# W_o and x kept in halves; attention results of two tiles loaded and combined before the projections end

## Chip, cores and metric

The kernel runs on one core of one Trainium2 chip. The metric is the device time of one execution in microseconds (us), the median of several runs.

## The reference

One inference step of a decoder layer: 2048 prompt rows (x_prompt) and 32 sample rows (8 requests of 4), width 1024. What matters here is the path from x to the mixer's output:

```python
qa, ka, va, qb, kb, vb, ga, gb = jnp.split(x @ w_in, SPLIT_POINTS, axis=-1)
# A: window 128, 8 query heads; B: (window, dilation) (128,1), (512,4), (2048,16)
oa = _band_values(p, va).reshape(n, t, A_Q)          # softmax with sinks
ob = _combine_groups(outs, lses)                     # three dilations, weighted by denominators
m = jax.nn.sigmoid(ga) * (oa @ w_br_a) + jax.nn.sigmoid(gb) * (ob @ w_br_b)
mix = m @ w_o
h = _layernorm(ALPHA * x + mix, ln1_g, ln1_b)
...
a = sum((conv_w[j] * ext[:, j:j + t] for j in range(CONV_W)), conv_b)
f = (jax.nn.gelu(a, approximate=False) * v) @ w_down
```

The sample rows attend to caches that are read from HBM. All is float32; outputs are the two y, the new cache rows and the convolution states.

## The kernel before

Every float32 operand of a product is split into a high part (ACT copies it, rounded) and a low part (DVE or GpSimd, called POOL, subtracts): `split`, lines 41 and 42. A product is then three matmuls, high by high, low by high and high by low.

**Phase 1** projects x. x is loaded, transposed on TensorE (PE) and kept whole in SBUF as one tile R, 128 partitions x 8 blocks of the width x 2048 rows. The work is a list of slots, `seq` in `phase1`, one slot per tile of 128 rows and per kind: B0, B1 and B2 (the three dilations of B), A, and G (the gates' last columns). The rows of a tile are a slice of R's columns: contiguous for B0, A and G, with stride 4 for B1 and stride 16 for B2. Each kind has 16 slots and one slot for the sample rows (number 16, which in G stands after slot 2). A slot runs four weight units of 256 columns (tile w), 96 matmuls into two banks psd (line 383); `make_xs` splits the x of the next slot (tile xs) at the slot's start. The banks are evicted by ACT (line 454, into a buffer b) in G and stored to d_gate by POOL's queue.

Everything else is threaded between the matmuls, eight points a slot: attention of the slot before, in G the sample attention (`sample_attn`, tiles V), and `wsteps`, a list of splits of the weights that come next. `pace` says how many splits run at each point (2 in G). Raw weights pass through the ten buffers b (`bufp`): `prefetch` issues their loads on SP up to `rawlim` pieces ahead, each of 256 KB, in a fixed order: w_in, then W_o in 16 pieces, the branch weights br in 12 (w_br_a's left half, w_br_b, w_br_a's right half, four each), then w_up. `loadcap` bounds how far. A split releases its buffer, and its step issues the next load.

**The passage to phase 2.** After G slot 13 `phase2_begin` opens the pool p2a and loads the attention results of tile 0: `load(0)` is nine DMAs on SP (oa; rb, the reciprocal denominators, into a buffer b; the weights wb; ob of the three dilations, strided) and `loadg` two (the gates ga). In slot 14, after the first unit, R is released and its place taken by WO (`phase2_weights`), 16 pieces to be split; after the third unit tile 0 is combined (`combine`: DVE weights and adds the dilations) and split into oT. In slot 15 the branch weights are split into the w tiles that the slot's units release; after its third unit come `load(1)` and the first sigmoids.

**Phase 2** goes over 16 prompt tiles and the sample tile: `mT(i-1)` transposes the gated sum m, `branches(i)` multiplies oT by the branch weights (four groups, 36 matmuls into psb, line 1089), DVE multiplies by the gates (line 1234) and POOL adds (line 1240, m), `oT(i+1)` is split, `outproj(i-1)` multiplies by WO (48 matmuls into psw, line 1089), and the layer norm follows. `combine(i+1)` stands in `branches(i)` between the gate products of its first and its second half. `load(i+1)` is issued at the start of iteration i. The tiles oa, wb, ob and oT have one buffer each, so load(i+1) waits until oT(i) has been made, and oT(i+1) until branches(i) has been read. **Phase 3** is the ConvFFN (psu, psdn) in four groups of rows.

Engines run in the order in which the program issues; SP's queue too.

Of the kernel before, what the change touches and what calls it, by code (L numbers as in the profile page):

```python
# [7 lines left out]
F32 = mybir.dt.float32  # L8
F32R = mybir.dt.float32r
# [7 lines left out]
SEQ = 2048  # L17
# [17 lines left out]
class Net:  # L35
# [142 lines left out]
    def phase1(self):  # L178
        nc, tc, a = self.nc, self.tc, self.a
        with ExitStack() as st:  # L180
            rp = ExitStack()
# [5 lines left out]
            self.R = self.pool(rp, "rp").tile([128, 8, SEQ], F32, name="R")  # L187
# [35 lines left out]
            for n, (kind, i, t) in enumerate(seq):  # L223
# [4 lines left out]
                self.pool_gate = kind == "G"  # L228
                nxt = seq[n + 1] if n + 1 < len(seq) else None
# [32 lines left out]
                if kind == "G" and i == 13:  # L262
                    assert not self.jobs, "sample attention is late"
                    sa.close()
                    self.phase2_begin()
                if kind == "G" and i in (12, 13):
                    if i == 12:
                        cc = self.conv_consts()
                    next(cc, 0)
# [61 lines left out]
    def trans_x(self, i):  # L331
        nc = self.nc
        xr = self.xr.pop(i)
        for h in range(2):
            ps = self.psT.tile([128, 512], F32, tag="t", name="pst")
            for k in range(4):
                nc.tensor.transpose(ps[:, k * 128:(k + 1) * 128], xr[h][:, k * 128:(k + 1) * 128], self.idn)
            nc.scalar.activation(self.R[:, 4 * h:4 * h + 4, i * 128:(i + 1) * 128],
                                 ps.rearrange("p (k t) -> p k t", k=4), AF.Copy)
# [9 lines left out]
    def make_xs(self, t, pool=False):  # L349
        xs = self.xsp.tile([128, 2, 8, 128], F32R, tag="xs", name="xs")  # L350
        self.split(xs[:, 0], xs[:, 1], self.R[:, :, t[1]], self.nc.gpsimd if pool else None)
        return xs

    def slot(self, kind, i, t, xs, units, prep, after_unit, rp):
        nc = self.nc
# [10 lines left out]
        if kind == "A" and i == 16:  # L366
            pace = (0, 0, 1, 1, 1, 1, 2, 2)
        if kind != "B0" or i > 0:
            out = prep()
        for half in range(2):  # L370
            ps = self.pd.tile([128, 512], F32, tag="d", name="psd")
            for uu in range(2):
# [23 lines left out]
                if u == 0 and kind == "G" and i == 14:  # L396
                    rp.close()
                    self.phase2_weights()
                after_unit(u)
                if kind == "G" and i == 14 and u == 2:  # L400
                    self.combine(0)
                    self.oT(0)
                if kind == "G" and i == 15 and u == 2:
                    self.load(1)
                if kind == "G" and i == 15 and u == 2:
                    self.sigmoid(0)
# [692 lines left out]
    def phase2_begin(self):  # L1099
        self.sta = ExitStack()  # L1100
        self.p2a = self.pool(self.sta, "p2a", side="right")
        self.S = {}
        self.load(0)
        self.loadg(0, 0)
        self.loadg(0, 1)

    def phase2_weights(self):

        self.wost = ExitStack()
        self.WO = self.pool(self.wost, "wop").tile([128, 2, 8, 1024], F32R, name="WO")  # L1110
        for c in range(4):
            cs = slice(c * 256, c * 256 + 256)
            self.wsteps += self.unit_steps((self.WO[:, 0, :, cs], self.WO[:, 1, :, cs]), True)[1]
# [7 lines left out]
    def load(self, i):  # L1121
# [3 lines left out]
        if M == 128:  # L1125
            d["oa"] = self.p2a.tile([128, 4, 128], F32, tag="oa", name="oa")
            nc.sync.dma_start(d["oa"], self.d_oa[:, r0:r0 + M].rearrange("(k p) t -> p k t", p=128))
            rb = self.buf()
            d["rb"] = rb.rearrange("p (c t) -> p c t", c=4)
# [65 lines left out]
    def phase2(self):  # L1195
# [17 lines left out]
        def branches(i):  # L1213
# [4 lines left out]
            for n in range(2):  # L1218
# [24 lines left out]
                if n == 0 and i < N - 1:  # L1243
                    self.combine(i + 1)
# [13 lines left out]
        def outproj(i):  # L1258
# [4 lines left out]
            for n in range(2):  # L1263
                cs = slice(n * 512, (n + 1) * 512)
                ps = psW.tile([128, 512], F32, tag="w", name="psw")
                for k in range(8):
                    self.split_mm(ps, M, t[:, 0, k], t[:, 1, k], WO[:, 0, k, cs], WO[:, 1, k, cs], k == 0, k == 7)
# [384 lines left out]
```

## Time and profile before

| | us |
|---|---|
| median of 3 runs | 3225.4 (3224.82 to 3226.73) |
| the profiled execution | 3227.46 |
| its span, first to last instruction | 3225.7 |
| PE busy with matmuls | 3157.8 (98%) |
| DVE busy | 1813.1 (56%) |
| ACT busy | 1419.3 (44%) |
| POOL busy | 747.1 (23%) |

PE's busy time is modelled to a matmul's end, so it doesn't tell full speed from a lower clock; the granted clock does, 0.994 in the mean of the span. Phase 1 ends at about 1297 us, phase 2 lies from 1299 to 1673, phase 3 behind. A row of a timeline gives start, duration, engine, line, operation, output and inputs; in brackets the idle time before it and what ended that. SPq is SP's queue of DMA issues.

### The profile page before, as it was taken

To read this page: it belongs to the slowest core of one execution; us is meant where nothing else is said; L and a number is where in the kernel's file an instruction comes from. 1 tells how busy PE (TensorE), PEld (TensorE's weight loads), DVE (VectorE), ACT (ScalarE), POOL (GpSimd) and SP (SyncE) were. 2 spreads that over 40 slices of the span, in tenths; PEclk is the share of its full clock that TensorE was granted. 3 is DMA by queue.
4 is the path that set the end of the run, shared out by engine and by line. 5 is a ranking of instruction groups with operands and counts; after the bars stand their busy time and mean duration, and the time that the engine had idled before them with its cause. 6 is when DMAs were issued, how large, how long until landed. Compare 5 with 4: busy or idle time off the path is not lost.

```text
span 3225.7 us, 56679 instructions
## 1 busy us (share of the span) xinstructions
PE 3157.8 (98%) x21839; PEld 2909.1 (90%) x21839; DVE 1813.1 (56%) x3694; ACT 1419.3 (44%) x3257; POOL 747.1 (23%) x783
## 2 busy tenths in 40 slices
PE   8999999999999999899999999999999999999998
PEld 8999998998999899688877988888888988999998
DVE  5656656656676532677765444564446444474446
ACT  6666666666666442322224233342343242342332
POOL 2114544654332201355540000020003000030001
PEclk9999999999999999899999999999999999999999
DMA  3113313413221344877735323443334333442231
GB/s 117 55 49 96 85 33 103 122 52 101 70 62 49 89 153 124 211 184 181 189 120 151 98 88 95 132 141 91 100 107 116 125 98 92 127 142 83 71 98 54
DMA packets 480548, 343.03 MB, mean 106 GB/s; under 512 B 114450, under 2 KB 436076, under 8 KB 480278
## 3 DMA queue, kind: packets, MB, share of 16 engines
q1 hardware_dynamic: 462390, 290.78, 31.7%
q0 software_dynamic: 17744, 48.56, 5.1%
q8 instruction: 172, 2.82, 0.4%
q14 instruction: 98, 0.80, 0.1%
q10 hardware_dynamic: 144, 0.07, 0.0%
HBM read 279.71 MB, written 59.59 MB: 105 GB/s over the span
## 4 chain that ended last, share of the span: by engine, by line
PE 67%; issue 6%; DVE 4%; ACT 3%; DMA 2%; POOL 1%; SPq 0%; DVEq 0%; POOLq 0%; ACTq 0%
PE psu L1411 31%; PE psdn L1089 14%; PE psd L383 8%; PE psw L1089 5%; PE psb L1089 4%; PE psdf L1089 1%; ACT P L721 1%; DVE w L42 1%; PE pst L566 1%; DMA oa<-d_oa 1%; PE pso L736 1%; DVE P L716 0%; PE pst L1253 0%; DVE b L575 0%; PE pss L636 0%
## 5 line engine op out<-in xcount | busy, mean ns | idle before, releaser
L1411 PE MATMUL psu<-h,w 128*128 128x512 f32 (+1 forms) x5280 | 1012.4, 353 | 2.8 <-ACT h L41 2.8
L383 PE MATMUL psd<-w,xs 128*128 128x256 f32 x7680 | 978.1, 284 | 21.1 <-DVE w L42 7.1
L1411 PEld LDWEIGHTS psu<-h,w 128*128 128x128 f32 x5280 | 860.3, 188 | 149.3 <-ACT h L41 3.8
L383 PEld LDWEIGHTS psd<-w,xs 128*128 128x128 f32 x7680 | 935.9, 190 | 28.2 <-ACT w L41 10.2
L1089 PE MATMUL psdn<-w,gt 128*128 128x256 f32 (+1 forms) x4008 | 474.9, 279 | 1.9 <-DVE y L1462 1.9
L1089 PEld LDWEIGHTS psdn<-w,gt 128*128 128x128 f32 (+1 forms) x4008 | 472.2, 186 | 4.9 <-DVE y L1462 4.1
L42 DVE TENSOR_TENSOR w<-b,w 128x512 fp32r<-128x512 f32 (+1 forms) x613 | 406.8, 722 | 19.2 <-ACT w L41 18.1
L41 ACT ACTIVATE w<-b 128x512 fp32r<-128x512 f32 x636 | 346.0, 607 | 126.5 <-PE psdn L1089 61.1
L1422 ACT ACTIVATE ext<-psu 128x512 f32<-128x512 f32 (+1 forms) x110 | 56.3, 512 | 452.1 <-PE psu L1411 452.0
L1435 DVE SCALAR_TENSOR_TENSOR ac<-ext,cw,ac 128x512 f32<-128x512 f32 (+1 forms) x88 | 71.2, 809 | 286.9 <-ACT ac L1434 286.9
L1431 POOL COPY mix<-ext 128x2 f32<-128x2 f32 x66 | 13.2, 199 | 926.6 <-ACT ext L1422 906.5
L1462 DVE SCALAR_TENSOR_TENSOR y<-y,psdn 128x256 f32<-128x256 f32 x176 | 73.1, 420 | 274.9 <-PE psdn L1089 271.5
L1089 PE MATMUL psw<-WO,mT 128*128 128x512 f32 (+1 forms) x800 | 189.4, 395 | 0.7 <-DVE mT L42 0.7
L1089 PEld LDWEIGHTS psw<-WO,mT 128*128 128x128 f32 (+1 forms) x800 | 148.5, 186 | 38.6 <-DVE mT L42 0.8
L42 DVE TENSOR_TENSOR PT<-pst,PT 128x512 fp32r<-128x512 f32 (+1 forms) x160 | 91.5, 608 | 154.4 <-ACT PT L41 153.7
L1089 PE MATMUL psb<-w,oT 128*128 128x512 f32 (+1 forms) x600 | 150.1, 409 | 6.7 <-ACT b L454 4.6
L41 ACT ACTIVATE gt<-ac 128x512 fp32r<-128x512 f32 x110 | 58.3, 549 | 222.0 <-DVE ac L1442 162.6
L1089 PEld LDWEIGHTS psb<-w,oT 128*128 128x128 f32 (+1 forms) x600 | 114.3, 193 | 35.9 <-ACT b L454 5.2
L42 POOL TENSOR_TENSOR xs<-R,xs 128x1024 fp32r<-128x1024 f32 x48 | 131.9, 2748 | 62.8 <-ACT xs L41 54.2
L683 POOL TENSOR_TENSOR b<-b 64x256 f32<-64x256 f32 x96 | 70.3, 733 | 271.1 <-DVE b L575 267.5
L42 DVE TENSOR_TENSOR xs<-R,xs 128x1024 fp32r<-128x1024 f32 x32 | 41.6, 1298 | 146.2 <-ACT xs L41 146.1
L41 ACT ACTIVATE xs<-R 128x1024 fp32r<-128x1024 f32 x80 | 115.8, 1447 | 0.9 <-ACT b L768 0.4
(253 smaller groups left out, 3689.5 us busy)
## 6 DMA issues: line engine op xcount, KB each, us to landing
b<-in_w_up SPq DMA_DIRECT2D x352, 256.0 KB, 3.9
b<-in_w_down SPq DMA_DIRECT2D x160, 256.0 KB, 3.5
b<-in_w_in SPq DMA_DIRECT2D x80, 256.0 KB, 4.5
b<-in_x_prompt SPq DMA_DIRECT2D x64, 256.0 KB, 3.9
b<-in_cache_b SPq DMA_DIRECT2D x64, 256.0 KB, 3.4
ga<-d_gate SPq DMA_DIRECT2D x32, 512.0 KB, 5.8
b<-d_q SPq DMA_DIRECT2D x48, 256.0 KB, 4.2
d_gate<-b SPq DMA_DIRECT2D x64, 128.0 KB, 2.0
```

Source lines behind the costliest of these rows:

```text
L41: self.nc.scalar.activation(hi, src, AF.Copy)
L42: (eng or self.nc.vector).tensor_tensor(lo, src, hi.bitcast(F32), ALU.subtract)
L383: nc.tensor.matmul(dst, lhsT=l, rhs=r[:, k, :], start=(k == 0 and q == 0), stop=(k == 7 and q == len(ops) - 1))
L566: nc.tensor.transpose(ps[:, n * 128:(n + 1) * 128], P[:, x, b * 128:(b + 1) * 128], self.idn)
L683: nc.gpsimd.tensor_tensor(o[:, :, 0], o[:, :, 0], o[:, :, 1], ALU.add)
L721: nc.scalar.activation(P[:, y, :nk + 1], P[:, y, :nk + 1], AF.Exp, bias=nm[:, c + y:c + y + 1], scale=SCALE, accum_out=den[:, c + y:c + y ...
L736: nc.tensor.matmul(ops[:, x * 256:(x + 1) * 256], lhsT=vs[b][:, x], rhs=PTs[x][:, q, b * 256:(b + 1) * 256], start=(b == 0 and q == 0), st ...
L1089: self.nc.tensor.matmul(ps[:x.shape[1]], lhsT=x, rhs=w, start=(first and q == 0), stop=(last and q == len(ops) - 1))
L1411: nc.tensor.matmul(ps[:, :b1 - b0], lhsT=w[:, k, c0:c0 + 128], rhs=h[:, x, k, b0:b1], start=(k == 0 and q == 0), stop=(k == 7 and q == 2))
L1422: nc.scalar.activation(ext[:, 2 + b0:2 + e1], ps[:, 0:e1 - b0], AF.Copy)
L1435: nc.vector.scalar_tensor_tensor(ac[:, :L], ext[:, 1:1 + L], cw[:, 1, j:j + 1], ac[:, :L], ALU.mult, ALU.add)
L1462: nc.vector.scalar_tensor_tensor(y[x][:M, cs], y[x][:M, cs], ALPHA if first else 1.0, ps[:M], ALU.mult, ALU.add)
```

## The change

R becomes two tiles of 1024 columns each (tags r0 and r1 of the pool rp), and so does WO: each half of WO takes the place of one half of R. `make_xs` splits a tile of rows half by half where it crosses. R's first half is last read for slot 7, so `wo_tile(0)` is made at the start of slot 8; its first two loads are issued at the start of slot 7, with rawlim 2 from there to slot 12 (before: 4), and its eight pieces are split at two points a slot. The second half is made in slot 14, as all of WO was before. The sample attention's pools are closed after slot 10 instead of 13, and load(0) follows there; `loadg(0, .)` stays after slot 13. Tile 0 is combined and split in slot 12, load(1) is issued in slot 13, combine(1) runs in slot 14 and is dropped from branches(0). rb gets a tile of its own in p2a.

The order of PE's instructions is the same. On SP, the loads between the sample attention's caches (in_cache_b, the V tiles) and the first norm rows stand thus before; WO's pieces are in_w_o:

```order
L947 DMA b<-in_cache_b 128x2x256 x32
L997 DMA b<-in_cache_a 128x4x128 x2
L112 DMA b<-in_w_o 128x2x256 x6
L1157 DMA b<-in_conv_w 22x3x128
L1158 DMA b<-in_conv_b 22x128
L1127 DMA oa<-d_oa 128x4x128
L1132 DMA b<-d_rec 64x4x128 x2
L1136 DMA wb<-d_w 64x6x128 x2
L1138 DMA ob<-d_ob 128x2x128
L1145 DMA ob<-d_ob 128x4x32 x2
L1145 DMA ob<-d_ob 128x16x8 x2
L1150 DMA ga<-d_gate 128x2x512 x2
```

They go on with the ten other pieces of W_o, the branch weights, two of w_up, load(1) (nine DMAs as above) and four of w_up. In the changed kernel the same place begins:

```order
L972 DMA b<-in_cache_b 128x2x256 x17
L112 DMA b<-in_w_o 128x2x256 x2
L972 DMA b<-in_cache_b 128x2x256 x10
L112 DMA b<-in_w_o 128x2x256
L972 DMA b<-in_cache_b 128x2x256 x2
L112 DMA b<-in_w_o 128x2x256
L972 DMA b<-in_cache_b 128x2x256 x3
L112 DMA b<-in_w_o 128x2x256
L1022 DMA b<-in_cache_a 128x4x128 x2
L112 DMA b<-in_w_o 128x2x256 x3
L1153 DMA oa<-d_oa 128x4x128
```

Eight pieces of W_o now stand among the last 15 V loads and behind them, and load(0) ahead of the conv constants. Behind the constants and load(1), where slot 14's loads begin, the row reads:

```order
L1175 DMA ga<-d_gate 128x2x512 x2
L112 DMA b<-in_w_o 128x2x256 x2
L112 DMA b<-in_w_br_a 128x512 x4
L112 DMA b<-in_w_br_b 128x512 x4
L112 DMA b<-in_w_br_a 128x512 x4
L112 DMA b<-in_w_up 128x4x128 x6
L1175 DMA ga<-d_gate 128x2x512 x2
```

Two pieces of W_o stand there instead of ten, and no load(1) between the w_up.

On DVE, from slot 14 to the first transposed sum (mT), the order before (wb is the combination, w the branch weights, ga the gate products of branches(0)):

```order
L42 TENSOR_TENSOR WO<-b,WO 128x2x256 x6
L42 TENSOR_TENSOR w<-b,w 128x512 x9
L1234 TENSOR_TENSOR ga<-psb,ga 128x512 x2
L1179 TENSOR_TENSOR wb<-ob,wb 128x256 x3
L1180 TENSOR_TENSOR wb<-wb 128x256
L1181 TENSOR_TENSOR wb<-wb 128x256
L1234 TENSOR_TENSOR ga<-psb,ga 128x512 x2
L1191 TENSOR_TENSOR oa<-oa,b 128x512
L42 TENSOR_TENSOR oT<-oa,oT 128x512
L42 TENSOR_TENSOR oT<-wb,oT 128x256
```

and now:

```order
L42 TENSOR_TENSOR WO<-b,WO 128x2x256 x6
L1204 TENSOR_TENSOR wb<-ob,wb 128x256 x3
L1205 TENSOR_TENSOR wb<-wb 128x256
L1206 TENSOR_TENSOR wb<-wb 128x256
L42 TENSOR_TENSOR w<-b,w 128x512 x9
L1259 TENSOR_TENSOR ga<-psb,ga 128x512 x4
L1216 TENSOR_TENSOR oa<-oa,rb 128x512
L42 TENSOR_TENSOR oT<-oa,oT 128x512
L42 TENSOR_TENSOR oT<-wb,oT 128x256
```

The combination of tile 1 stands ahead of the branch weights' splits, and the four gate products of tile 0 follow each other.

```diff
@@ -184,7 +184,9 @@
             self.psT = self.pool(st, "psT", bufs=3, space=PSUM)
             self.psO = self.pool(st, "psO", bufs=1, space=PSUM)
             self.bgq, self.wsteps = [], []
-            self.R = self.pool(rp, "rp").tile([128, 8, SEQ], F32, name="R")
+            self.rp = self.pool(rp, "rp")
+            self.R = [self.rp.tile([128, 8, SEQ // 2], F32, tag="r%d" % h, name="R") for h in range(2)]
+            self.wost = rp
             self.xss = self.cpx.tile([128, 8, 64], F32R, name="xss")
             self.sqT = self.cpx.tile([128, 4, 4, NS], F32, name="sqT")
             self.skT = self.cpx.tile([128, 4, 2, NS], F32, name="skT")
@@ -226,6 +228,11 @@
                     self.loadcap += 16 if kind != "G" else 10 ** 6
                     self.prefetch(6)
                 self.pool_gate = kind == "G"
+                if kind == "G" and i == 7 and t[0] == "p":
+                    self.loadcap += 8
+                    self.prefetch(2)
+                if kind == "G" and i == 8:
+                    self.WO = [self.wo_tile(0)]
                 nxt = seq[n + 1] if n + 1 < len(seq) else None
                 nextp = [q for q in seq[n + 1:n + 3] if q[1] < 16][:1]
                 newunits = []
@@ -259,10 +266,13 @@
                 if i == 16 and kind != "G":
                     if kind != "A":
                         self.bgq.append(self.sample_scores(self.gcol[kind][0]))
-                if kind == "G" and i == 13:
+                if kind == "G" and i == 10:
                     assert not self.jobs, "sample attention is late"
                     sa.close()
                     self.phase2_begin()
+                if kind == "G" and i == 13:
+                    self.loadg(0, 0)
+                    self.loadg(0, 1)
                 if kind == "G" and i in (12, 13):
                     if i == 12:
                         cc = self.conv_consts()
@@ -335,7 +345,7 @@
             ps = self.psT.tile([128, 512], F32, tag="t", name="pst")
             for k in range(4):
                 nc.tensor.transpose(ps[:, k * 128:(k + 1) * 128], xr[h][:, k * 128:(k + 1) * 128], self.idn)
-            nc.scalar.activation(self.R[:, 4 * h:4 * h + 4, i * 128:(i + 1) * 128],
+            nc.scalar.activation(self.R[i // 8][:, 4 * h:4 * h + 4, i % 8 * 128:(i % 8 + 1) * 128],
                                  ps.rearrange("p (k t) -> p k t", k=4), AF.Copy)
 
     def xs_sample(self):
@@ -348,7 +358,17 @@
 
     def make_xs(self, t, pool=False):
         xs = self.xsp.tile([128, 2, 8, 128], F32R, tag="xs", name="xs")
-        self.split(xs[:, 0], xs[:, 1], self.R[:, :, t[1]], self.nc.gpsimd if pool else None)
+        s, e, d = t[1].start, t[1].stop, t[1].step or 1
+        at = 0
+        for h, R in enumerate(self.R):
+            o = h * (SEQ // 2)
+            lo, hi = max(s - o, 0) if s >= o else (s - o) % d, min(e - o, SEQ // 2)
+            if lo >= hi:
+                continue
+            n = (hi - lo - 1) // d + 1
+            self.split(xs[:, 0, :, at:at + n], xs[:, 1, :, at:at + n], R[:, :, slice(lo, lo + (n - 1) * d + 1, d)],
+                       self.nc.gpsimd if pool else None)
+            at += n
         return xs
 
     def slot(self, kind, i, t, xs, units, prep, after_unit, rp):
@@ -365,6 +385,8 @@
                 pace = (0, 0, 1, 1, 2, 2, 2, 2)
         if kind == "A" and i == 16:
             pace = (0, 0, 1, 1, 1, 1, 2, 2)
+        if kind == "G" and 8 <= i < 14:
+            pace = (0, 0, 1, 0, 0, 1, 0, 0)
         if kind != "B0" or i > 0:
             out = prep()
         for half in range(2):
@@ -394,14 +416,17 @@
                 if u == 1 and kind == "B0" and i == 0:
                     out = prep()
                 if u == 0 and kind == "G" and i == 14:
-                    rp.close()
                     self.phase2_weights()
                 after_unit(u)
-                if kind == "G" and i == 14 and u == 2:
+                if kind == "G" and i == 12 and u == 2:
                     self.combine(0)
                     self.oT(0)
-                if kind == "G" and i == 15 and u == 2:
+                if kind == "G" and i == 13 and u == 0:
                     self.load(1)
+                if kind == "G" and i == 14 and u == 2:
+                    self.combine(1)
+                if kind == "G" and i == 15 and u == 0:
+                    self.rawlim = 6
                 if kind == "G" and i == 15 and u == 2:
                     self.sigmoid(0)
             if smp:
@@ -1101,16 +1126,17 @@
         self.p2a = self.pool(self.sta, "p2a", side="right")
         self.S = {}
         self.load(0)
-        self.loadg(0, 0)
-        self.loadg(0, 1)
 
     def phase2_weights(self):
 
-        self.wost = ExitStack()
-        self.WO = self.pool(self.wost, "wop").tile([128, 2, 8, 1024], F32R, name="WO")
-        for c in range(4):
+        self.WO.append(self.wo_tile(1))
+
+    def wo_tile(self, h):
+        W = self.rp.tile([128, 2, 8, 512], F32R, tag="r%d" % h, name="WO")
+        for c in range(2):
             cs = slice(c * 256, c * 256 + 256)
-            self.wsteps += self.unit_steps((self.WO[:, 0, :, cs], self.WO[:, 1, :, cs]), True)[1]
+            self.wsteps += self.unit_steps((W[:, 0, :, cs], W[:, 1, :, cs]), True)[1]
+        return W
 
     def norm_rows(self, g, b):
         t = self.xsp.tile([128, 2, 1024], F32, tag="xs", name="gb")
@@ -1125,8 +1151,7 @@
         if M == 128:
             d["oa"] = self.p2a.tile([128, 4, 128], F32, tag="oa", name="oa")
             nc.sync.dma_start(d["oa"], self.d_oa[:, r0:r0 + M].rearrange("(k p) t -> p k t", p=128))
-            rb = self.buf()
-            d["rb"] = rb.rearrange("p (c t) -> p c t", c=4)
+            d["rb"] = self.p2a.tile([128, 4, 128], F32, tag="rb", name="rb")
             for s in range(2):
                 src = self.d_rec[i * 8 + s:i * 8 + 8:2, :].rearrange("(o c) t -> o c t", o=1)
                 nc.sync.dma_start(d["rb"][s * 64:(s + 1) * 64], src.to_broadcast([64, 4, 128]))
@@ -1240,7 +1265,7 @@
                 nc.gpsimd.tensor_tensor(m[:M, cs], ga[:M, 0], ga[:M, 1], ALU.add)
                 if i + 1 < N:
                     self.loadg(i + 1, n)
-                if n == 0 and i < N - 1:
+                if n == 0 and 0 < i < N - 1:
                     self.combine(i + 1)
 
         def mT(i):
@@ -1264,7 +1289,7 @@
                 cs = slice(n * 512, (n + 1) * 512)
                 ps = psW.tile([128, 512], F32, tag="w", name="psw")
                 for k in range(8):
-                    self.split_mm(ps, M, t[:, 0, k], t[:, 1, k], WO[:, 0, k, cs], WO[:, 1, k, cs], k == 0, k == 7)
+                    self.split_mm(ps, M, t[:, 0, k], t[:, 1, k], WO[n][:, 0, k], WO[n][:, 1, k], k == 0, k == 7)
                 nc.vector.scalar_tensor_tensor(z[n][:M], z[n][:M], ALPHA, ps[:M], ALU.mult, ALU.add)
                 if M != 128:
                     lo = self.lower(ps, M)
```

## The prediction

> **What bounds the kernel now.** I read the page first: TensorE (PE) is busy for 98% of the span, so a change can only win where PE waits or runs at a lower clock. Then I asked who waited for whom on PE in the stretch that the change touches, the passage from the projections (line 383, tile psd) to the branch and output products of phase 2 (line 1089, tiles psb and psw).
>
> ```profile
> span 3225.7 us, 56679 instructions
> ```
>
> The waits of PE between 1270 and 1360 us, with total, count and longest:
>
> ```profile
> PE pst L1253 <- POOL m L1240: 8.1, 2, 7.9
> PE psb L1089 <- ACT b L454: 4.6, 2, 2.5
> PE psb L1089 <- ACT oT L41: 1.9, 1, 1.9
> PE psd L383 <- ACT b L454: 1.3, 1, 1.3
> PE psb L1089 <- DVE oT L42: 0.2, 1, 0.2
> ```
>
> They add up to 16.1 us. The timeline of PE shows where they lie (in brackets the idle time before a row):
>
> ```profile
> 1272.65 17.30 PE L383 MATMUL psd<-w,xs 128*128 128x256 f32 x144
> 1291.26 5.95 PE L383 MATMUL psd<-w,xs 128*128 128x256 f32 x48 [1.31 <-ACT b L454]
> 1299.24 6.01 PE L1089 MATMUL psb<-w,oT 128*128 128x512 f32 x18 [2.04 <-ACT b L454]
> 1307.78 4.46 PE L1089 MATMUL psb<-w,oT 128*128 128x512 f32 x18 [2.53 <-ACT b L454]
> 1312.44 0.66 PE L1253 MATMUL pst<-idn,m 128*128 128x128 f32 x4 [0.19 <-POOL m L1240]
> 1320.98 1.11 PE L1253 MATMUL pst<-idn,m 128*128 128x128 f32 x4 [7.89 <-POOL m L1240]
> 1321.74 11.05 PE L1089 MATMUL psb<-w,oT 128*128 128x512 f32 x36
> 1332.63 11.36 PE L1089 MATMUL psw<-WO,mT 128*128 128x512 f32 x48
> 1343.83 1.03 PE L1253 MATMUL pst<-idn,m 128*128 128x128 f32 x8
> 1346.75 0.49 PE L1089 MATMUL psb<-w,oT 128*128 128x512 f32 x1 [1.88 <-ACT oT L41]
> 1347.47 9.98 PE L1089 MATMUL psb<-w,oT 128*128 128x512 f32 x35 [0.23 <-DVE oT L42]
> ```
>
> What the same work costs undisturbed stands one tile later in the chain of work that ended last (start, duration):
>
> ```profile
> 1368.66 0.87 PE pst L1288 x8
> 1369.53 0.97 PE pst L1253 x8
> 1370.50 8.39 PE psb L1089 x36
> 1378.90 11.20 PE psw L1089 x48
> ```
>
> So the passage can be priced. From 1289.95 (the end of the 144 projections) to 1368.66 it took 78.7 us. Its work, undisturbed: 48 projections at 17.30/144 us, 5.8; three branch tiles, 3 x 8.39; two output tiles, 2 x 11.20; two sets of transposes, 2 x 0.97. That makes 55.3, so **23.4 us are lost**: 16.1 idle and 7.3 of matmuls that ran slower. The windows of 4 us (the second-last group of numbers begins with the granted clock) show why:
>
> ```profile
> 1300.00:1304.00 4.00, 4.00 (x13) 3.15 (x12) 2.54 (x3) 2.47 (x4) 1.33 (x2) 0.61 0.80 231
> 1308.00:1312.00 4.00, 4.00 (x18) 3.08 (x17) 2.73 (x4) 0.77 (x2) 2.07 (x3) 1.00 1.20 219
> 1348.00:1352.00 4.00, 4.00 (x13) 3.14 (x12) 3.93 (x9) 1.86 (x2) 0.57 (x1) 0.63 0.72 196
> ```
>
> After the idle 2.04 us the clock is 0.61, after the idle 1.88 and 0.23 it is 0.63; after the idle 2.53 it stays at 1.00. In the same rows the DMA engines are full (0.80, 1.20, 0.72). The whole loss belongs to one crowding: from slot 14 on, ten pieces of W_o, twelve of the branch weights, six of w_up and the attention results of tile 1 go through SP, ACT and DVE at once, and the combination of tile 1 stands on DVE between the two pairs of gate products of tile 0.
>
> **The change part by part.** *W_o's first half early.* Eight pieces (8 x one ACT, six DVE, two POOL splits) leave slots 14 and 15 and go to slots 8 to 11, two a slot. The room there, and the price of a split:
>
> ```profile
> 1250.00:1261.00 11.00, 11.00 (x96) 11.00 (x95) 1.23 (x1) 1.84 (x3) 1.08 (x2) 1.00 0.21 72
> ```
>
> ```profile
> L41 ACT ACTIVATE w<-b x12: 613/618/632, 1294.2 to 1308.2; 128x512 fp32r<-128x512 f32 x12
> ```
>
> A slot of 11 us has ACT busy 1.84 and DVE 1.23 us there, so two splits of 0.62 us cost nothing; in slots 8 and 9, which also run sample attention, the V tiles are the cover, priced with the rivals. What it frees is ACT's queue: in slots 14 and 15 the evictions of psd (ACT b L454) stand behind eight fewer splits, and the branch weights, now directly behind W_o's second half, come about eight transfers sooner. That should end the waits of 1.31, 2.04 and 2.53 us with the slow clock behind them (6.01 + 4.46 against 8.39, 2.1 us): 8.0 us. They could all stay (0) or all go (8.0). I take 7.0, since the weight tiles only come free as slot 15's own units end, and the transfers are slow here:
>
> ```profile
> b<-in_w_br_a SPq DMA_DIRECT2D x8, 256.0 KB, 6.0
> ```
>
> *Tile 0's and 1's attention results early.* load(0) moves from the end of slot 13 to that of slot 10, load(1) from slot 15 to slot 13; each carries nine DMAs on SP. Moved past: the six prefetched W_o pieces, conv constants and the gate loads, all without a waiter on PE before slot 14. combine(1) leaves the middle of branches(0). Its price shows in these rows of DVE and POOL:
>
> ```profile
> 1317.92 1.28 DVE L1234 TENSOR_TENSOR ga<-psb,ga 128x512 f32<-128x512 f32 x2
> 1319.12 0.68 DVE L1191 TENSOR_TENSOR oa<-oa,b 128x512 f32<-128x512 f32 x1
> 1320.56 0.92 DVE L42 TENSOR_TENSOR oT<-oa,oT 128x512 fp32r<-128x512 f32 x1 [0.76 <-ACT oT L41]
> ```
>
> ```profile
> 1319.29 1.64 POOL L1240 TENSOR_TENSOR m<-ga 128x512 f32<-128x512 f32 x1 [6.91 <-DVE ga L1234]
> ```
>
> Without it the last gate product (0.64) follows the last psb matmul at once, POOL's sum of 1.28 to 1.64 follows that, and the second four transposes come 2.1 to 2.4 us after psb instead of 8.7. **A wait remains**: nothing else is there for PE, and oT of tile 1 is no sooner, as its one buffer is read until psb(0) ends: 0.64 + 0.68 + 0.76 + part of 0.92, about 2.8 us from psb's end to the next branch matmul, of which 0.97 is transposes. So 1.9 us stay idle of 8.1, a gain of 6.2.
>
> *The clock behind it.* In the kernel before psb(1) took 11.05 us, 2.7 over 8.39, behind the 7.89 idle. Behind an idle of 1.9 us the near rows are 0 (after 2.53) and 2.1 (10.47 against 8.39 at 1347). I take 2.1, as two of the three idles near 2 us were followed by the lower clock: a gain of 0.6. The Trainium skill, "TensorE: Matmul & The Clock Gate", Part 1 on the HAM clock gate, says that the clock drops after an idle window of about 3.4 us; by that rule this term would be a gain of 2.7. The rows at 0.61 and 0.63 speak against the rule as a bound for a single gap, and I go by them.
>
> *Tile 2, the next to be late.* Its transfers can't start before oT(1) has read the buffers:
>
> ```profile
> 1300.89 1.69 SPq L1127 DMA_DIRECT2D oa<-d_oa  x1
> ...
> 1321.64 0.56 SPq L1127 DMA_DIRECT2D oa<-d_oa  x1
> ```
>
> ```profile
> 1316.60 0.61 DVE L1179 TENSOR_TENSOR wb<-ob,wb 128x256 f32<-128x256 f32 x1 [1.92 <-DMA ob<-d_ob]
> ...
> 1339.17 0.68 DVE L1179 TENSOR_TENSOR wb<-ob,wb 128x256 f32<-128x256 f32 x1 [2.57 <-DMA ob<-d_ob]
> ```
>
> From the second issue to the first psb of tile 2 (1346.75) passed 25.1 us. Afterwards: projections end at 1289.95 + 5.8 = 1295.7; psb(0) at 1304.1; oT(1) and so the issue at 1306.8; psb(1) 10.5, psw(0) 11.2, transposes 0.97: PE is ready for tile 2 at 1329.6, 22.8 us after the issue. With the old 25.1 it would wait 2.3 and, by the row at 0.63, pay 2.1 for the clock; with four w_up pieces fewer right ahead of it in the queue perhaps nothing. Of the present 4.2 us (1.88 + 0.23 + 2.1) I take 1.5 as staying: a gain of 2.7.
>
> *The rest of the 23.4* (8.0 + 8.1 + 2.7 + 4.2 are 23.0), slow matmuls of psd and psw, goes with its causes: 0.4.
>
> *R in two halves.* Only the tiles of kind B2 (stride 16) cross the halves: 16 tiles with two ACT and two POOL instructions instead of one.
>
> ```profile
> L42 POOL TENSOR_TENSOR xs<-R,xs x18: 2396/2924/2952, 478.6 to 732.3; 128x1024 fp32r<-128x1024 f32 x18
> L41 ACT ACTIVATE xs<-R x17: 1064/1987/2027, 490.1 to 731.2; 128x1024 fp32r<-128x1024 f32 x17
> ```
>
> Two contiguous splits of 512 (0.62 each) against one of 1024 (1.06) show what cutting costs, about 0.2 us a tile: nothing at best, 16 x 0.2 = 3.2 us if all of it were on the path. xs is made a slot ahead, and the slots are (732.3 - 478.6)/17 = 14.9 us apart, against 1.99 + 2.92 for the two splits; I take 0.5, near the lower end.
>
> **Sum**: 7.0 + 6.2 + 0.6 + 2.7 + 0.4 - 0.5 = 16.4 us. The profiled execution took 3227.46 us (span 3225.7), 2.1 above the median of 3225.4; 3227.46 - 16.4 = 3211.1, and set against the median **3209.0**. A measurement of this kernel tells about 0.2% (6.5 us) from no change.
>
> **The rivals.**
> *No slow clock behind the remaining gap* (as after the idle 2.53): 2.1 better, 3206.9. The page named above would have it so. Chance 0.14.
> *The wait moves to tile 2*: load(2) takes the old 25.1 us, so 4.4 stay instead of 1.5, and a little of the branch weights' wait: 3212. For it: load(2) still goes through behind w_up, gates and norm rows. Chance 0.18.
> *The branch weights stay late*: then 1.31 + 2.04 + 2.53 + 2.1 stay in place of 1.0, 7.0 less: 3216. Against it: eight fewer transfers ahead of them. Chance 0.12.
> *The change doesn't do what it says*: load(1) lands late and combine(1) holds DVE in slot 14, ahead of the branch splits, as long as it did in branches(0): 3222. It has from slot 13's first quarter to slot 14's third, 17 us (a slot is 96 projections, 11.5 us); it took 15.7 before (1300.89 to 1316.60). Chance 0.08.
> *Slower*: W_o's pieces stand between sample attention's V loads in SP's queue and hold two of its ten buffers.
>
> ```profile
> L947 SPq DMA_DIRECT2D b<-in_cache_b x32: 367/368/421, 1134.5 to 1200.4; - x32
> DMA to landing us min/median/max: 2.6/3.0/4.9
> ```
>
> ```profile
> L41 ACT ACTIVATE V<-b x40: 400/632/636, 1133.6 to 1215.5; 128x512 fp32r<-128x512 f32 x32, 128x256 fp32r<-128x256 f32 x8
> ```
>
> The last load is issued 15.1 us before its split. If that lead fell below the landing time of 3.0 to 4.9 us, each of the 15 V tiles loaded behind the first two W_o pieces would stop PE for what a landing of 3.0 us is longer than the 2.1 us between splits ((1215.5 - 1133.6)/39), 0.9 us, and a lower clock could cost as much again: 15 x 1.8 = 27 against the gain of 16.4, or 3236. Two buffers of ten take only about a fifth of the lead (12 us left). Chance 0.04.
>
> **How the numbers follow.** Forecast 0.44, rivals 0.14, 0.18, 0.12, 0.08, 0.04. Faster by over 0.2% (under 3218.9): 0.44 + 0.14 + 0.18 + 0.12 = 0.88. Same: 0.08. Slower: 0.04. The range 3204.5 to 3218.0 reaches from all waits gone but the 1.9 us (23.4 - 1.9 - 0.6) to the late branch weights with 2 us more.
>
> **What would show it.** Right: no PE wait on ACT b L454 near the end of phase 1; one wait of about 2 us on POOL's m in place of 7.89; the first psb of tile 2 at 1329 to 1332 us; PE without waits in slots 7 to 13 and in B2. Wrong: psb waits for ACT w or its transfers (third rival), DVE idle for ob in slot 14 (fourth), PE waits on V tiles (fifth), or more PE time in the B2 windows than before.

## The result and the profile after

The changed kernel takes 3208.44 us (median of 4 runs, 3207.07 to 3210.24) against 3225.11 us before in the same comparison (4 runs, 3223.86 to 3226.73): ratio 0.9950, interval 0.9939 to 0.9962, so 16.7 us or 0.52% faster. The profiled execution took 3208.9 us, its span is 3206.8 us.

The waits of PE between 1270 and 1360 us after the change (total, count, longest):

```profile
PE pst L1278 <- POOL m L1265: 2.1, 1, 2.1
PE psb L1114 <- ACT oT L41: 1.7, 1, 1.7
PE psb L1114 <- DVE oT L42: 0.2, 1, 0.2
```

4.0 us are left of 16.1; ACT's b no longer appears, and m costs 2.1 in place of 8.1. Where they lie, in PE's timeline after:

```profile
1272.56 22.98 PE L405 MATMUL psd<-w,xs 128*128 128x256 f32 x192
1295.38 8.56 PE L1114 MATMUL psb<-w,oT 128*128 128x512 f32 x36
1303.78 0.60 PE L1278 MATMUL pst<-idn,m 128*128 128x128 f32 x4
1306.45 0.66 PE L1278 MATMUL pst<-idn,m 128*128 128x128 f32 x4 [2.07 <-POOL m L1265]
1306.86 8.65 PE L1114 MATMUL psb<-w,oT 128*128 128x512 f32 x36
1315.35 11.36 PE L1114 MATMUL psw<-WO,mT 128*128 128x512 f32 x48
1326.55 1.04 PE L1278 MATMUL pst<-idn,m 128*128 128x128 f32 x8
1329.25 0.50 PE L1114 MATMUL psb<-w,oT 128*128 128x512 f32 x1 [1.66 <-ACT oT L41]
1329.97 8.43 PE L1114 MATMUL psb<-w,oT 128*128 128x512 f32 x35 [0.23 <-DVE oT L42]
...
1349.44 1.03 PE L1313 MATMUL pst<-idn,b 128*128 128x128 f32 x8
```

All 192 projections of the last two slots run in one piece, and each branch tile takes 8.6 to 8.9 us: the granted clock is 1.00 over the whole stretch. I call the stretch from the start of those projections to the transposes of b (line 1313 here, 1288 before) the **passage**. It took 1368.50 - 1272.65 = 95.9 us before (1368.50 is that row's start in PE's timeline, 1368.66 in the chain) and takes 1349.44 - 1272.56 = 76.9 now. The 19.0 us between them are all that the two profiled executions differ by (spans 3225.7 and 3206.8).

### The profile page after: what moved, and what is told of

It is laid out like the page before. It is cut to its first block, busy times and chain, and to the rows that moved or that the text cites. A ratio compares the mean times of both kernels' runs of the same rounds, so it can differ in the third digit from the quotient of the medians.

```text
span 3206.8 us, 56702 instructions
## 1 busy us (share of the span) xinstructions
PE 3151.4 (98%) x21839; PEld 2904.2 (91%) x21839; DVE 1811.1 (56%) x3694; ACT 1420.2 (44%) x3273; POOL 749.0 (23%) x799
## 4 chain that ended last, share of the span: by engine, by line
PE 73%; DVE 4%; ACT 3%; issue 2%; DMA 1%; POOL 1%; SPq 0%; DVEq 0%; POOLq 0%; ACTq 0%
PE psu L1436 31%; PE psdn L1114 15%; PE psd L405 13%; PE psw L1114 4%; PE psb L1114 4%; PE psdf L1114 1%; ACT P L746 1%; PE pst L591 1%; DVE w L42 1%; PE pso L761 1%; PE pso L1008 1%; DVE P L741 0%; PE pss L661 0%; DVE b L600 0%; PE pst L1278 0%
## 5 line engine op out<-in xcount | busy, mean ns | idle before, releaser
L42 DVE TENSOR_TENSOR PT<-pst,PT 128x512 fp32r<-128x512 f32 (+1 forms) x160 | 91.6, 608 | 155.9 <-ACT PT L41 155.2
L42 POOL TENSOR_TENSOR xs<-R,xs 128x1024 fp32r<-128x1024 f32 (+1 forms) x64 | 134.8, 2115 | 50.9 <-ACT xs L41 45.6
L41 ACT ACTIVATE xs<-R 128x1024 fp32r<-128x1024 f32 (+1 forms) x96 | 117.8, 1246 | 0.9 <-ACT b L793 0.4
```

The costliest lines, as they stand in the source:

```text
L41: self.nc.scalar.activation(hi, src, AF.Copy)
L42: (eng or self.nc.vector).tensor_tensor(lo, src, hi.bitcast(F32), ALU.subtract)
```

## The experiments

Times are medians; before was 3225.3 us beside halves_only, attn_late, wo_late and combine_back, and 3224.4 beside the other four, so a difference across the two sets carries those 0.9 us. A ratio's interval is some 0.0012 (4 us) to either side, too wide to part neighbours, so the table adds two readings of the profiled execution: the passage, and PE's idle time in it. What is left after the idle time and the undisturbed work (the prediction's 55.3 us and the 144 projections at 17.30, 72.6 together) is matmuls at a low clock, within 0.8 us: in wo_late, after, ups_later and ob_early the granted clock over the passage is 1.00, and the working leaves -0.2 to 0.8.

| kernel | median us | passage | idle | low clock |
|---|---|---|---|---|
| before | 3225.3 / 3224.4 | 95.9 | 16.1 | 7.2 |
| halves_only | 3225.4 | 91.6 | 14.9 | 4.1 |
| load0_only | 3220.7 | 87.0 | 11.4 | 2.9 |
| attn_late | 3218.2 | 84.4 | 9.7 | 2.1 |
| load1_late | 3214.3 | 82.3 | 7.7 | 2.0 |
| wo_late | 3212.0 | 79.0 | 5.6 | 0.8 |
| combine_back | 3209.8 | 77.3 | 3.4 | 1.3 |
| after | 3208.4 | 76.9 | 4.0 | 0.3 |
| ups_later | 3208.8 | 74.4 | 2.1 | -0.2 |
| ob_early | 3206.5 | 75.2 | 2.4 | 0.2 |

**halves_only**: the kernel before, with R and W_o in two tiles each.

```diff
-self.R = self.pool(rp, "rp").tile([128, 8, SEQ], F32, name="R")
+self.R = [self.rp.tile([128, 8, SEQ // 2], F32, tag="r%d" % h, name="R") for h in range(2)]
...
+self.WO = [self.wo_tile(0), self.wo_tile(1)]
```

> The kernel before, with R and W_o in two halves each and the split of xs cut where a tile crosses them; nothing is loaded or combined earlier. Theory: 0.5 us more than before, 3225.6, and not over 3226.5. Rival 1: the cut splits of the 16 tiles of kind B2 are on the path, 3.2 us more, 3228.3. Rival 2: W_o's first half can start sooner since its half of R is free from slot 7 on, and some us are gained without moving anything: 3222 or less.

Ratio 0.9999 (0.9990 to 1.0009): neither 3.2 us of cut splits nor a gain. The halves are an enabler without a measurable price. The passages of the two kernels, which do the same work there, differ by 4.3 us, 3.1 of it low clock: so far off can the passage of one execution be.

**wo_late**: the changed kernel with both halves of W_o in slot 14.

```diff
...
-    self.prefetch(2)
-if kind == "G" and i == 8:
-    self.WO = [self.wo_tile(0)]
...
-self.WO.append(self.wo_tile(1))
+self.WO = [self.wo_tile(0), self.wo_tile(1)]
```

> The changed kernel, but W_o's first half is loaded and split with the second in slots 14 and 15, as before the change; the early attention results stay. Theory (the prediction's term): the evictions of psd on ACT and the branch weights are late again, PE waits on ACT b and for the branch weights near 1290 to 1310 us, 7.0 us with the slow clock: 3215.4 us, between 3213 and 3217. Rival 1, the attention results alone carry the gain: at most 2 us, 3210.5 or less. Rival 2, the two crowdings feed each other, so that either alone brings most of the loss back: 12 us or more, 3220.5 or above.

3.5 us worse by the medians, 2.1 by the passage, 1.9 by the ratios (0.9956 against 0.9950): between the theory (7.0) and rival 1. Of the waits on ACT's b, 5.9 us before, only one of 1.4 is back. PE's timeline of wo_late:

```profile
1301.30 4.46 PE L1109 MATMUL psb<-w,oT 128*128 128x512 f32 x18 [1.39 <-ACT b L474]
```

**attn_late, load1_late, load0_only**: the attention moves undone in steps. attn_late has load(0), the gate loads and combine(0) in slots 13 and 14, load(1) in slot 15 and combine(1) in branches(0), with W_o early. load1_late leaves load(0) and combine(0) early. load0_only is load1_late with W_o late. The edit that they share:

```diff
-if kind == "G" and i == 13 and u == 0:
+if kind == "G" and i == 15 and u == 2:
     self.load(1)
-if kind == "G" and i == 14 and u == 2:
-    self.combine(1)
...
-if n == 0 and 0 < i < N - 1:
+if n == 0 and i < N - 1:
     self.combine(i + 1)
```

> The changed kernel, but load(0), the gate loads, combine(0), load(1) and combine(1) stand where they stood before the change; W_o's first half stays early. Theory (the prediction's terms 6.2, 0.6 and 2.7): PE waits about 8 us on POOL's m and some 2 us more at tile 2, 9.5 us: 3218 us, between 3215 and 3220. Rival 1: with eight W_o pieces out of SP's queue load(1) lands in time even from slot 15, and the wait on m stays near 2 us: at most 3 us, 3211.5 or less. Rival 2, the crowdings feed each other: 13 us or more, 3221.5 or above.

> The changed kernel, but load(1) stands in slot 15 and combine(1) in branches(0) again; load(0), combine(0) and W_o's first half stay early. Theory (the time of load(1) is what the attention move is worth): the wait on POOL's m is 7 us again with a low clock behind it, tile 2 some 0.5 us later, as with all attention work late: 3218 us, not under 3215. Rival (tile 0's early combination frees buffers and queues, so load(1) lands earlier even from slot 15): half of it, 3211 to 3214, and SP issues load(1) by 1292 us without waiting.

> The kernel before with the halves and with load(0), the gate loads and combine(0) early; W_o and load(1) late. Theory (the two crowdings share ACT, DVE and SP in slots 14 and 15, and taking tile 0's attention work away ends most of PE's waits on ACT b): those waits fall from 5.9 to about 1.4 us, the wait on m stays 7 to 8 us: 3219 us, between 3217 and 3221. Rival (the waits on ACT b ended because load(1)'s transfers left slot 15): they stay near 5.9 us, 3223 or more.

attn_late's time came as the theory had it (9.8 against 9.5 us), with 7.3 us of wait on m and 1.5 of low clock behind it. load1_late gave back 5.9 us, close to its rival (3214, issue by 1292 us) and far from the theory; load0_only met its theory, waits on b of 1.7 us, and 3220.7.

With after and wo_late they tell what each step is worth, by medians and in brackets by passages. W_o early: 6.3 us (4.7) with load(1) late, 3.5 (2.1) with load(1) early; load(0) is early in both. load(0) early: 3.9 (2.1) with W_o early. load(1) early: 8.7 (8.0) with W_o late, 5.9 (5.5) with W_o early. The single steps add up differently by order, because they relieve the same queue: W_o's pieces also stand ahead of load(1), whose first transfer goes out at 1297.40 in load0_only and at 1292.41 in load1_late.

Two steps from the kernel before hold more than their own edit. All kernels but before and halves_only keep rb's own tile and the deeper prefetch of slot 15 (rawlim 6). So W_o early with all attention work late, 7.1 us (3225.3 to 3218.2), and load(0) early with W_o late, 3.7 to 4.6, contain these. SP's queue shows what the tile does: before (here rb's buffer is b),

```profile
1249.21 0.39 SPq L1127 DMA_DIRECT2D oa<-d_oa  x1
1264.94 1.35 SPq L1132 DMA_DIRECT2D b<-d_rec  x2
...
1273.00 2.05 SPq L1150 DMA_DIRECT2D ga<-d_gate  x2
1275.21 11.49 SPq L112 DMA_DIRECT2D b<-in_w_o  x10
1288.74 4.35 SPq L112 DMA_DIRECT2D b<-in_w_br_a  x4
```

and in load0_only:

```profile
1266.85 17.67 SPq L112 DMA_DIRECT2D b<-in_w_o  x10
1284.75 4.34 SPq L112 DMA_DIRECT2D b<-in_w_br_a  x4
```

SP's waits before (total, count, longest) say what it stood for inside load(0), a buffer that a store of the gates still read:

```profile
SPq L1132 <- DMA d_gate<-b: 15.2, 1, 15.2
```

Then it issued load(0)'s other transfers and the gate loads for 10 us, ahead of W_o. In load0_only the ten pieces go out 8.4 us sooner and the branch weights 4.0 us sooner. attn_late has the tile and leaves load(0) where it was:

```profile
1253.00 4.24 SPq L1168 DMA_DIRECT2D ob<-d_ob  x4
...
1266.38 4.54 SPq L112 DMA_DIRECT2D b<-in_w_o  x2
1272.93 6.27 SPq L112 DMA_DIRECT2D b<-in_w_br_a  x4
```

There load(0) waits for no buffer and is issued by 1257.24, and W_o's last pieces and the branch weights start at 1266.38 and 1272.93; in load1_late, with load(0) early too, they start at 1265.02 and 1272.87. So what takes load(0)'s ten us out of the weights' way is rb's own tile, and the earlier slot adds 1.4 and 0.1 us. No run moves rb alone, and what its tile is worth in time stays open.

Late weights reach PE through ACT. Before the change ACT waits for a branch weight, splits it, and only then evicts the bank for which PE's first psb waits until 1299.24:

```profile
1298.08 0.63 ACT L41 ACTIVATE w<-b 128x512 fp32r<-128x512 f32 x1 [0.88 <-DMA b<-in_w_br_a]
1298.61 0.58 ACT L454 ACTIVATE b<-psd 128x512 f32<-128x512 f32 x1
```

PE's waits on ACT's b are 5.9 us before, 1.7 in load0_only and none in attn_late.

How load(1) sets the wait on m is seen on SP and DVE of load1_late:

```profile
1292.41 0.58 SPq L1151 DMA_DIRECT2D oa<-d_oa  x1
...
1297.22 6.02 SPq L1168 DMA_DIRECT2D ob<-d_ob  x4
```

```profile
1305.87 0.61 DVE L1202 TENSOR_TENSOR wb<-ob,wb 128x256 f32<-128x256 f32 x1 [1.52 <-DMA ob<-d_ob]
...
1307.19 1.28 DVE L1257 TENSOR_TENSOR ga<-psb,ga 128x512 f32<-128x512 f32 x2
```

The issue alone takes 10.8 us (1292.41 to 1303.24), the last product of combine(1) waits for the last transfer, and the gate products of psb(0), ready since 1304, stand behind it. PE then waits 5.67 us on m.

**combine_back**: only combine(1)'s place undone; load(1) stays in slot 13.

```diff
-if kind == "G" and i == 14 and u == 2:
-    self.combine(1)
...
-if n == 0 and 0 < i < N - 1:
+if n == 0 and i < N - 1:
```

> The changed kernel, but combine(1) stands in branches(0) again, between the two pairs of gate products; load(1) stays in slot 13. Theory of the prediction as worded (combine(1)'s place costs): PE's wait on POOL's m grows from 2.1 to 5 us or more, and tile 2 comes later: 3 to 8 us, 3211.5 to 3216.5. Rival (only the time of load(1) counts): the transfers have landed, combine(1)'s some 2 us of DVE fit between the two psb pairs, 4.2 us apart, and the time is that of the changed kernel, 3208.4 within 1.2 us, with the wait on m still near 2 us.

PE's timeline of combine_back:

```profile
1307.74 0.66 PE L1276 MATMUL pst<-idn,m 128*128 128x128 f32 x4 [3.42 <-POOL m L1263]
1308.15 10.19 PE L1112 MATMUL psb<-w,oT 128*128 128x512 f32 x36
...
1330.16 8.63 PE L1112 MATMUL psb<-w,oT 128*128 128x512 f32 x36
```

Both were half right. The wait on m grew by 1.35 us and a low clock of 1.6 followed it, but the waits at tile 2 vanished: its first psb starts at 1330.16, where that of the changed kernel starts at 1329.25 and goes on at 1329.97. The passage is 0.5 us longer, the time 1.4, inside the spread. combine_back and load1_late differ in nothing but the time of load(1): that is worth 4.5 us by the medians and 5.0 by the passages. So most of what paid is the time of load(1), not the place of combine(1). What the place is worth alone stays open: load(2) goes out 1.3 us later in combine_back (1308.26 against 1306.97), yet oT(2) is ready 1.5 us sooner (its last split starts at 1328.31 against 1329.84), since DVE has the last ob 11.9 us after the first issue in place of 14.7. Why these transfers were quicker isn't shown; without that the place would have cost more than 0.5 us.

**ups_later and ob_early**: that chain shortened. ups_later splits the first w_up pieces after oT(2); ob_early does so too and issues the five transfers of ob for tile 2 in slot 15.

```diff
-if i == 1:
-    self.ups = [self.next_unit()]
 if i + 1 < N:
     self.oT(i + 1)
+if i == 1:
+    self.ups = [self.next_unit()]
```

```diff
 if kind == "G" and i == 15 and u == 0:
     self.rawlim = 6
+    self.load_ob(2)
```

> The changed kernel, but the first four pieces of w_up are split after oT(2) instead of before it. Theory (the wait at tile 2 is load(2)'s chain with 3.59 us of splits on DVE inside it): the waits of 1.66 and 0.23 us at tile 2 go, 1.9 us, 3206.5 us, in the trace at the first psb of tile 2. Rival (the transfers of load(2) set the end alone): the waits stay and the time is 3208.4; or the splits, moved, make a later product wait and nothing is gained.

> As the kernel with the w_up pieces split after oT(2), and besides the five transfers of ob for tile 2 are issued in slot 15, since combine(1) has read that buffer by then. Theory: combine(2) no longer waits for ob at 1318 to 1322 us, tile 2 is ready over 4 us earlier than PE asks for it, and only the wait of 2.1 us on POOL's m remains: 3206.5 us. Rival: the five transfers stand ahead of w_up and the gates in a full queue and hold those up, nothing gained or up to 2 us lost, 3208.4 to 3210.5.

What stands ahead of oT(2) on DVE in the changed kernel:

```profile
1321.68 0.67 DVE L1204 TENSOR_TENSOR wb<-ob,wb 128x256 f32<-128x256 f32 x1 [2.34 <-DMA ob<-d_ob]
...
1324.26 3.59 DVE L42 TENSOR_TENSOR w<-b,w 128x512 fp32r<-128x512 f32 x4
1327.77 0.68 DVE L1216 TENSOR_TENSOR oa<-oa,rb 128x512 f32<-128x512 f32 x1
```

In ups_later both waits at tile 2 are gone, as the theory has it, and the passage is 2.5 us shorter; but its median is 3208.8 and shows nothing of it. In the profiled execution, the slowest of its five (3210.07), phase 1 ended 2.8 us later (the 192 projections start at 1275.36), so a gain of 2 us sits inside the spread between executions. ob_early's passage is 1.7 us shorter, and its median 3206.54 (3205.64 to 3211.12) is the lowest of all kernels; its ratio, 0.9948 (0.9936 to 0.9961), doesn't part it from the changed kernel's 0.9950. The rival's price is there as well, a new wait of 0.5 us on ACT's b.

**gaps_a to gaps_d**: the clock. Behind the branch products of tiles 2 to 15 PE is made to wait for copies of a psum tile, on DVE (a, b) or ACT (c, d), of 14 lengths in two orders. Each of the four ran once.

```diff
+def gap(i, ps):
+    gp = p2a.tile([128, 512], F32, tag="gp", name="gp")
+    for w in gaps[i]:
+        nc.vector.tensor_copy(gp[:, :w], ps[:, :w])
+    pt = psT.tile([128, 512], F32, tag="t", name="pstg")
+    nc.tensor.transpose(pt[:64, :128], gp[:, :64], self.idn)
```

> The changed kernel, with one idle gap of PE made on purpose behind the branch products of each of the tiles 2 to 15: DVE copies a psum tile, 0.1 to 3.7 us of copies after the gate product, and PE transposes the copy. The result is untouched; the time is longer by the gaps. Theory of the prediction (an idle near 2 us is followed by the low clock in two cases of three, a longer one surely): slow matmuls behind most gaps from 2 us up. Rival 1 (a threshold near 3.4 us): none behind gaps under 3.4, some behind every gap over it. Rival 2 (it hangs on where the gap falls in time): between about 1.5 and 4 us some gaps are followed by it and others of the same length not, more often the longer they are.

> The same gaps in another order over the tiles. Theory of the prediction: the same lengths give the same answer, low clock from about 2 us up. Rival 1: the same lengths give the same answer, from 3.4 us up. Rival 2: lengths in the middle change their answer with the tile they stand at.

> The changed kernel with a gap of PE behind the branch products of tiles 2 to 15, this time made with 0.2 to 2.5 us of copies on ACT, which is mostly idle there, so that the gaps lie between about 0.6 and 3.5 us. The longer gaps made with DVE (3.2 to 8.2 us) were all followed by slow matmuls, 1.3 to 2.8 us of them. Rival 1 (a threshold near 3.4 us): nothing behind any of these. Rival 2 (it hangs on where the gap falls in time): nothing below about 1.7 us, some of those from 1.7 to 3.2 us, all above. Theory of the prediction: most from 2 us up.

> The same gaps made with ACT, in another order over the tiles. Rival 2 expects that some lengths between 1.7 and 3.2 us change their answer; rival 1 none at all; the theory of the prediction that a length gives the same answer in both.

The experiment missed its aim in part: both engines had work of their own in front, and of 56 gaps 54 came out over 3 us (3.18 to 8.15). All 54 were followed by slow matmuls, psw taking 12.7 to 14.2 us in place of 11.36, and the excess, 1.3 to 2.8 us, doesn't grow with the gap: 1.33 behind 7.81 us, 2.78 behind 4.87 (gaps_a). The two others, set beside the wait of 2.04 before the change, speak against both the theory and rival 1. gaps_c and gaps_d, at one place of the program:

```profile
1717.54 0.30 PE L1280 MATMUL pstg<-idn,gp 128*64 128x128 f32 x1 [2.73 <-ACT gp L1278]
1717.60 12.98 PE L1114 MATMUL psw<-WO,mT 128*128 128x512 f32 x48
```

```profile
1716.34 0.30 PE L1280 MATMUL pstg<-idn,gp 128*64 128x128 f32 x1 [2.41 <-ACT gp L1278]
1716.39 11.43 PE L1114 MATMUL psw<-WO,mT 128*128 128x512 f32 x48
```

A gap of 2.73 is followed by the low clock, so a bound of 3.4 us for a single gap is wrong; 2.41 isn't, and before the change 2.04 was, so length alone doesn't settle it. More is in the windows of 0.5 us around the low clock of the kernel before (the second-last group begins with the granted clock):

```profile
1299.50:1300.00 0.50, 0.50 (x3) 0.35 (x3) 0.26 (x1) 0.50 (x2) 0.50 (x1) 0.73 0.78 262
...
1303.00:1303.50 0.50, 0.50 (x4) 0.42 (x3) 0.50 (x1) 0.50 (x1) 0.00 (x0) 0.85 0.98 362
...
1347.50:1348.00 0.50, 0.50 (x1) 0.46 (x2) 0.50 (x2) 0.50 (x2) 0.00 (x0) 0.52 0.00 0
```

Away from such edges the clock is either 1.00 or 0.50, so a mean of 0.73 puts the fall at 1299.73; by the same working it rises at 1303.15 and falls again at 1347.52. The low clock lasts 3.42 us, and 1347.52 - 1299.73 = 47.79 is 14 times 3.413. So the falls and rises lie on a grid of 3.41 us, which runs on whatever the program does. In each of seven profiles read so (before, after, halves_only, combine_back, attn_late, load1_late, load0_only) every change of the clock between 200 and 1400 us lies on one such grid within 0.02 us, and the grid lies elsewhere in each execution. Cut along the grid, the windows of the kernel before are (PE's busy time is the first number behind the length):

```profile
1296.32:1299.73 3.41, 1.38 (x10) 1.13 (x9) 2.92 (x4) 2.29 (x5) 0.72 (x2) 1.00 0.98 319
1299.73:1303.15 3.42, 3.42 (x10) 2.64 (x9) 2.33 (x3) 1.89 (x4) 1.60 (x2) 0.50 0.73 192
1303.15:1306.56 3.41, 2.11 (x9) 1.36 (x8) 0.47 (x1) 3.40 (x4) 0.00 (x0) 1.00 1.10 367
1306.56:1309.97 3.41, 2.19 (x9) 1.80 (x10) 2.38 (x4) 2.21 (x5) 1.78 (x2) 1.00 1.21 205
```

and those of the changed kernel:

```profile
1301.90:1305.31 3.41, 2.48 (x13) 1.81 (x11) 1.98 (x3) 0.00 (x0) 1.58 (x2) 1.00 0.46 150
1305.31:1308.72 3.41, 2.27 (x12) 2.00 (x13) 2.45 (x4) 3.00 (x6) 1.09 (x1) 1.00 1.00 268
```

The idle 2.04 us lay in one window, which was busy for 1.38 of 3.41 us (40%), and the next window ran at half clock. The idle 2.53 was cut by the grid at 1306.56 into windows of 62 and 64%, and nothing followed. The 2.07 us after the change were cut at 1305.31 (73 and 67%), and nothing followed. Over the seven profiles, from 200 us on, a window at full clock that was busy for 45% or less was always followed by the low clock, one of 56% or more never. Of the 16 between, 5 were followed by it; the busiest of these 5, at 55%, is in load0_only, and the clock behind it is 0.50:

```profile
283.29:286.70 3.41, 1.88 (x13) 1.47 (x12) 3.41 (x3) 2.26 (x6) 2.49 (x2) 1.00 0.00 0
```

What decides between 46 and 55% no run shows.

## Why the prediction was right

The time, 3208.4 against 3209.0 us forecast, and the direction were right. Term by term, in the passages of the two profiled executions:

- *W_o's first half early*, 7.0 of 8.0: the stretch gained all 8.0. As a cause the term was too large. Beside early attention work the edit is worth 3.5 us (wo_late against after), and the 7.1 of attn_late against before contain rb's own tile. The prediction counted W_o's eight transfers ahead of the branch weights; it left out load(0)'s ten us of issue, which the wait for rb's buffer had pushed in front of them too. The third rival, 7.0 us worse if the weights stayed late, was priced too high for the same reason: in wo_late 1.4 us of these waits are back.
- *combine(1) leaves the middle of branches(0)*, 6.2 of 8.1: 6.0, the wait that remains is 2.1 against 1.9. The size was right, the reason named only in a small part. The wait on m falls in steps: 8.1 before, 7.3 with W_o early and rb's tile (attn_late), 5.7 with load(0) early too (load1_late), 3.4 with load(1) early too (combine_back), and 2.1 when combine(1) moves. The last step is the one that the prediction named; it is 1.3 us, and the passage is 0.5 us shorter for it.
- *The clock behind it*, 0.6 of 2.7: all of it. The timeline gives an undisturbed branch tile 8.65 us, where the prediction set its 11.05 against 8.39 of the chain, so 2.4 us were there to gain. The assumption that 2.1 us of low clock stay failed in the profiled execution. The prediction read a length into three idles near 2 us; the grid decides. By it a gap of 2.07 us leaves a window busy for 45% or less (1.88 us idle or more) in (3.41 - 2.07 + 2 x 0.19) / 3.41 = 50% of positions, and one of 55% or less in 71%. That is an estimate from the rows above, and not far from the two in three of the prediction; another execution of the same kernel may pay it. The rival of 3206.9 has the right profile, by luck of the grid. The Trainium skill, "TensorE: Matmul & The Clock Gate", Part 1, calls the window free-running and 3413 ns long, and the trace agrees (3.41); its idle window of about 3.4 us isn't needed as a gap, as 2.04 us in one window of 40% show.
- *Tile 2*, 2.7 of 4.2: 2.3, the idle 1.66 and 0.23 stay where 1.5 were forecast. load(2) went out at 1306.97 (forecast 1306.8) and the first psb came 22.3 us later, where the old path took 25.1. The prediction added this wait to the low clock ahead of it, and the two replace each other: a psb(1) slower by 1.6 to 2.1 us would have brought PE to tile 2 at 1329.2 to 1329.7 in place of 1327.6, when oT(2) was all but ready. So the rival's 2.1 us for a full clock were too many. That is worked out from PE's rows; no run shows it alone.
- *The rest*, 0.4, came with them. *R in two halves*, -0.5, is too small to see (halves_only): two cut splits on POOL take 2 x 1.57 us against 2.90 for one, 0.24 more a tile (0.2 were forecast), and PE is busy for 223.2 us between 500 and 730 us before and after.

Their sum is 19.0 us in the passage, against 16.9 forecast without the halves; most of the difference is the clock term. The medians gained 16.7. The profiled execution of before was 2.1 us above its median, as the prediction said, so part of the 19.0 belongs to that one execution, and that the forecast of the median hit within 0.6 us is luck in part.

None of the other rivals came: PE has no wait between 1090 and 1272 us, so none on V tiles; DVE's combine(1) runs at 1282.63 without a wait for ob; the branch weights come in time. *The wait moves to tile 2* happened in small, 1.9 us.

## What to carry to other kernels

Before pricing an edit that empties a queue, count everything that stands in that queue ahead of the waiter, and ask what each entry itself waits for: here a buffer for one small transfer held up all that stood behind it. Two edits that relieve the same queue don't add, and in this case the first one made is worth most. A delay ahead of a wait for another chain doesn't add to that wait either: it takes its place, as far as the wait is long. When a wait ends on a combined result, ask whether its place on the engine or its transfer is late, and undo them one at a time. In this case gaps of TensorE were cheap while a window of 3.4 us held less than 1.5 us of idle time (56% busy); over that, what follows can cost as much as the gap.

## What the hardware showed

In seven profiles the clock of TensorE changed only on a grid of 3.41 us, fixed within an execution and different in the next; a window busy for 45% or less was paid for with the next one to three at half clock, 1.3 to 2.8 us behind the made gaps however long they were. So an execution gains or loses some us by luck: halves_only has a passage 4.3 us shorter than before's and the same median.

SP takes 8 to 13 us to issue the nine transfers of one load(i) (1249.11 to 1257.24 in attn_late, 1300.89 to 1313.8 before), and in load1_late the last product that needs them ran 2.6 us behind the last issue: this load was late mostly by its issue.

One stretch far behind the change, 400 psdn matmuls near 2900 us, takes either 45.61 or 47.31 us, with no idle time and a full clock in either. Before, after, combine_back and ob_early show the first, the other six of the table the second. No edit touches it, and it stays unexplained. Spans of single executions compare no better than these 1.7 us.
